# Opening of a conformer/attention block: x in eight wide transfers, true transposes, rstd at the read of the banks, shift and scale summed by one wide VectorE operation

## Chip, cores and metric

One core of one Trainium2 chip runs the kernel. The metric is the device time of one launch in microseconds (us), lower being better. The time given for the kernel before is the median of three runs; one more execution was taken with the hardware profiler.

## What is computed

The layer normalises x (512 tokens x 2048 features), modulates it by shift and scale that come from a conditioning vector c, multiplies it with one wide weight matrix, runs a convolution branch and an attention branch on the results, and merges them. The part that the change touches is the first five lines:

```python
c_act = jax.nn.silu(c)
mod = c_act @ w_ada[l] + b_ada[l]                 # 2048 -> 3 * 2048
shift, scale, gate = jnp.split(mod, 3, axis=-1)
h = rms_norm(x, g_pre[l]) * (1.0 + scale[:, None, :]) + shift[:, None, :]
p = h @ w_in[l]
cv, cg, cz, q, k, v, az, m_conv, m_attn = jnp.split(p, offsets, axis=-1)
y_conv = conv_branch(cv, cg, cz, conv_w[l], conv_b[l], cn_g[l], cn_b[l], w_conv_out[l])
y_attn = attn_branch(q, k, v, az, l, lam_q1[l], lam_k1[l], lam_q2[l], lam_k2[l], subln_g[l], w_attn_out[l])
merged = jax.nn.sigmoid(m_conv) * y_conv + jax.nn.sigmoid(m_attn) * y_attn
out = merged @ w_o[l]
x = x + gate[:, None, :] * rms_norm(out, g_post[l])
```

`rms_norm` divides each token by the root of its mean square (here rstd is one over that root) and multiplies by a vector over the features. Everything is float32.

## The kernel before

**Products.** A float32 operand is held as two parts of a shorter type, hi and lo, and a product is three matmuls (hi hi, hi lo, lo hi), issued by `mm3` (L161 to L167; the profile lists them under L163). `split` makes the parts: ScalarE rounds to hi (L141), VectorE takes the difference lo (L142). Features lie on the partitions, the 512 tokens in the free dimension; `h[k]` is the hi and lo tile of the 128 features of tile k, of 16.

**Opening, up to the first `pv` matmul.** x comes as tokens x features in 16 tiles of 128x512 (L93 to L95). `squares` (L211) sums the squares of the tiles, half on ScalarE and half on VectorE; `scales` (L221) makes rstd of two token tiles and a diagonal matrix with it. `norm_x` (L232) multiplies a piece of x with that diagonal on TensorE (L236), which transposes and scales it at once, and ScalarE copies the result from the PSUM bank to `xn` (L239): 64 products and 64 copies of 128x128.

Shift and scale of a few features at a time, a group, come from `ada` (L257). `GROUPS` (L47) gives seven of them: first column, width, and how many of the 16 parts of the sum over c TensorE takes; VectorE takes the rest. `ada_load` (L249) loads columns of `w_ada`, shift and scale apart, 512 KB each. On TensorE a part is a matmul with the vector c as the stationary operand, into `pa` (L273); on VectorE it is a scaled add into `acc` (L276, L278). Small matmuls turn the sums so that features lie on the partitions (`pm`, L288 to L294), and then ScalarE forms `hf` = xn * scale + shift (L305) and `split` makes `h[k]`.

`conv_gemm` (L318) multiplies the tiles `h[k]` of a group with the 2048 columns of the GLU part of `w_in`: one, one, two, two, two, four and four tiles k (kt0, kt1, kt2, kt4, kt6, kt8 and kt12 in what follows, by their first tile). The bank of each output tile (`pc`) goes to `part`: by a ScalarE copy for kt0 (L337), by a VectorE add for the others (L339), 16 per block. So a block needs its group's shift and scale, and while it runs, the next group's are worked out. `interleave` (L173) writes the two in alternating order, `ST` (L45) saying in how many steps, and the rest of `norm_x` is spread over kt0.

**Order.** All DMAs are issued by SyncE, in order. Inside the `manual_schedule` block (L349 to L364) instructions keep the order written; elsewhere a scheduler of the language orders each engine's program at build time. Each engine runs its program strictly in that order, so an instruction that waits holds everything behind it.

**Pools.** `page` (L69) hands out 59 tiles of 128x512; the loads of `ada` share seven tiles of 128x1024 (`AR`).

Behind the opening come the convolution taps on VectorE, attention, the gates and the two projections, whose TensorE program is the same before and after the change.

Of the kernel before, what the change touches and what calls it, by code (L numbers as in the profile page):

```python
# [977 lines left out]
```

## Time and profile before

| what | before |
|---|---|
| median of three runs | 1447.2 us (1445.42 to 1449.49) |
| profiled execution, its own time | span 1448.4 us |
| TensorE (PE) busy | 1413.6 us, 98% |
| VectorE (DVE) busy | 1053.0 us, 73% |
| ScalarE (ACT) busy | 534.2 us, 37% |
| bytes moved by DMA | 238.62 MB, 165 GB/s in the mean |
| first conv product / first `pv` product | 33.05 us / 258.29 us |

The profile gives busy time for each engine, and for TensorE the clock that it was granted as a share of full speed. A busy TensorE may be a slow one; matmuls overlap, so the distance from one start to the next is what one costs. Time lies on the path only where the engine that ends last waits for it.

### The profile page before, as it was taken

The numbers are of one execution on the slowest core, as the hardware profiler recorded it, in microseconds if no ns is written. First come the engines' busy times: TensorE is split into PE (matmuls) and PEld (weight loads), VectorE is DVE, ScalarE is ACT, GpSimd is POOL, SyncE is SP. The second block draws the span as 40 slices with busy tenths as digits, with TensorE's granted clock in tenths as the row PEclk, the third lists the DMA queues.
The fourth block names the chain that finished last, engine by engine and source line by source line (L and its number), as shares of the span: only waits on it lengthen the run. The fifth ranks groups of instructions, "written<-read, shape, count | busy, mean of one in ns | idle before, by whom it ended". The sixth has DMA issues, their size and how long they took to land.

```text
span 1448.4 us, 20732 instructions
## 1 busy us (share of the span) xinstructions
PE 1413.6 (98%) x8191; PEld 1200.4 (83%) x8191; DVE 1053.0 (73%) x1720; ACT 534.2 (37%) x901; POOL 1.8 (0%) x8
## 2 busy tenths in 40 slices
PE   4999999999999999999999999999999999999997
PEld 4776778787777877688999999999998888888885
DVE  4466785988888888588997888877767448656645
ACT  4622233223444244434544444444445323222230
POOL 0000000000000000000000000000000000000000
PEclk9999999999999999999999999999999999999999
DMA  9878653232223323124654555533369647267543
GB/s 285 264 255 291 215 167 130 88 131 87 66 81 102 102 67 109 66 95 135 209 165 160 187 178 191 188 121 132 126 226 349 224 137 233 95 207 243 189 145 145
DMA packets 178466, 238.62 MB, mean 165 GB/s; under 512 B 7793, under 2 KB 118722, under 8 KB 177474
## 3 DMA queue, kind: packets, MB, share of 16 engines
q1 hardware_dynamic: 178370, 237.31, 49.5%
q8 instruction: 64, 1.05, 0.3%
q14 instruction: 32, 0.26, 0.1%
HBM read 210.02 MB, written 27.26 MB: 164 GB/s over the span
## 4 chain that ended last, share of the span: by engine, by line
PE 93%; DVE 3%; DMA 1%; ACT 1%; issue 1%; SPq 0%; DVEq 0%; ACTq 0%
PE pc L163 12%; PE pw L163 12%; PE py_ya L163 6%; PE py_yc L163 6%; PE pv L163 6%; PE pg_k L163 6%; PE pg_q L163 5%; PE pg_az L163 5%; PE x_ma L163 5%; PE x_mc L163 5%; PE y_mc L163 3%; PE z_mc L163 3%; PE z_ma L163 3%; PE y_ma L163 3%; PE x_cz L163 2%; PE y_cz L163 2%
## 5 line engine op out<-in xcount | busy, mean ns | idle before, releaser
L468 DVE SCALAR_TENSOR_TENSOR cacc<-u,cw,cacc 128x511 f32<-128x511 f32 (+14 forms) x240 | 164.4, 729 | 0.0
L163 PE MATMUL pc<-hh,wh_c 128*128 128x512 f32 x256 | 102.9, 408 | 1.1 <-ACT hh L141 1.1
L163 PE MATMUL pc<-hh,wl_c 128*128 128x512 f32 x256 | 101.0, 398 | 1.5 <-DVE wl_c L142 1.4
L163 PE MATMUL pc<-hl,wh_c 128*128 128x512 f32 x256 | 101.7, 397 | 0.0
L339 DVE TENSOR_TENSOR part<-pc,part 128x512 f32<-128x512 f32 x96 | 66.0, 691 | 46.9 <-PE pc L163 45.8
L163 PE MATMUL pw<-wh_o,mh 128*128 128x512 f32 x224 | 89.0, 397 | 0.0
L163 PE MATMUL pw<-wh_o,ml 128*128 128x512 f32 x224 | 87.3, 390 | 0.0
L163 PE MATMUL pw<-wl_o,mh 128*128 128x512 f32 x224 | 87.2, 389 | 0.0
L141 ACT CAST wh_c<-wr_c 128x1024 fp32r<-128x1024 f32 (+1 forms) x36 | 34.6, 960 | 112.5 <-PE pc L163 85.6
L141 ACT CAST wh_o<-wr_o 128x1024 fp32r<-128x1024 f32 x28 | 29.5, 1053 | 104.5 <-PE pw L163 93.0
L163 PEld LDWEIGHTS pc<-hh,wh_c 128*128 128x128 f32 x256 | 49.0, 192 | 17.9 <-issue 3.3
L856 DVE SCALAR_TENSOR_TENSOR accg<-adag,cact,accg 128x512 f32<-128x512 f32 x60 | 45.0, 750 | 24.0 <-DMA adag<-in_w_ada_dram 22.8
L163 PEld LDWEIGHTS pc<-hh,wl_c 128*128 128x128 f32 x256 | 49.1, 192 | 15.7 <-issue 2.5
L142 DVE TENSOR_TENSOR wl_o<-wr_o,wh_o 128x1024 fp32r<-128x1024 f32 x28 | 34.2, 1221 | 34.0 <-ACT wh_o L141 34.0
L163 PEld LDWEIGHTS pc<-hl,wh_c 128*128 128x128 f32 x256 | 49.3, 192 | 10.2 <-issue 0.4
L163 PE MATMUL pv<-wh_v,hh 128*128 128x512 f32 x128 | 51.2, 400 | 0.9 <-DVE part L339 0.9
L142 DVE TENSOR_TENSOR wl_c<-wr_c,wh_c 128x1024 fp32r<-128x1024 f32 (+1 forms) x36 | 39.7, 1104 | 16.5 <-ACT wh_c L141 16.4
L163 PE MATMUL pg_q<-hh,wh_q 128*128 128x512 f32 x128 | 51.1, 399 | 0.0
L163 PE MATMUL pg_k<-hh,wl_k 128*128 128x512 f32 x128 | 51.1, 399 | 0.0
L163 PE MATMUL pg_q<-hl,wh_q 128*128 128x512 f32 x128 | 50.9, 397 | 0.0
L163 PE MATMUL pg_az<-hl,wh_az 128*128 128x512 f32 x128 | 50.7, 396 | 0.0
L163 PE MATMUL pv<-wl_v,hh 128*128 128x512 f32 x128 | 50.6, 395 | 0.0
(358 smaller groups left out, 4312.7 us busy)
## 6 DMA issues: line engine op xcount, KB each, us to landing
ada<-in_w_ada_dram SPq DMA_DIRECT2D x64, 512.0 KB, 6.1
wr_ma<-in_w_in_dram SPq DMA_DIRECT2D x16, 1024.0 KB, 5.5
wr_mc<-in_w_in_dram SPq DMA_DIRECT2D x16, 1024.0 KB, 5.0
adag<-in_w_ada_dram SPq DMA_DIRECT2D x32, 512.0 KB, 4.2
wr_o<-in_w_o_dram SPq DMA_DIRECT2D x16, 1024.0 KB, 5.1
wr_c<-in_w_in_dram SPq DMA_DIRECT2D x28, 512.0 KB, 5.0
wr_v<-in_w_in_dram SPq DMA_DIRECT2D x8, 1024.0 KB, 5.2
wr_q<-in_w_in_dram SPq DMA_DIRECT2D x8, 1024.0 KB, 5.3
```

Of the source, the lines that this page charges most:

```text
L141: nc.scalar.copy(hi, src)
L142: i = nc.vector.tensor_tensor(lo, src, hi.bitcast(F32), op=ALU.subtract)
L163: mm = nc.tensor.matmul(ps, a[p], b[q], start=start and i == 0, stop=stop and i == 2, skip_group_check=more)
L339: nc.vector.tensor_tensor(part[i], ps[f], part[i], op=ALU.add)
L468: paced(nc.vector.scalar_tensor_tensor(cvo[t][:, s:], u[t][:, :S - s], wj, cvo[t][:, s:], op0=ALU.mult, op1=ALU.add))
L856: nc.vector.scalar_tensor_tensor(acc, raw[:, k, :], s1, acc, op0=ALU.mult, op1=ALU.add)
```

## The change

- x comes in eight transfers of 128x1024 (512 KB), and the two row loads (`b_ada`, `g_pre`) behind them.
- `turn` transposes a piece of x with the identity; a broadcast of rstd over the partitions, made once by four small matmuls with a matrix of ones (`rsb`), is multiplied in by VectorE when it reads the bank: 64 transposes, four to a bank, and 16 VectorE operations of 128x512.
- A load of `ada` is one tile with shift and scale side by side, filled by two transfers of 256 KB. VectorE's part of a sum is one operation over both, twice as wide.
- `GROUPS`: the groups at columns 256 and 768 go from 16 parts on TensorE to none, that at 1024 from 12 to 8.
- Tiles that belong together (x, most of `xn`, hi and lo of `h`, `ya`, `mg`, `mgs`) are pairs of a pool of their own. The pages go from 59 to 27, the load tiles from 7 to 6.
- The small loads for the convolution and for lambda go behind the last load of `ada`.

```diff
-NPAGE = 59
+NPAGE = 27
-AR = 7
-ST = (3, 6, 6, 6, 13, 10)
-GROUPS = ((0, 128, 16), (128, 128, 16), (256, 256, 16), (512, 256, 16), (768, 256, 16),
-          (1024, 512, 12), (1536, 512, 0))
+AR = 6
+ST = (3, 10, 10, 10, 13, 10)
+GROUPS = ((0, 128, 16), (128, 128, 16), (256, 256, 0), (512, 256, 16), (768, 256, 0),
+          (1024, 512, 8), (1536, 512, 0))
...
     for t in range(NT):
-        for j in range(4):
-            nc.sync.dma_start(out=xs[t][j], in_=x2[t * P:(t + 1) * P, j * 512:(j + 1) * 512])
-        if t == 0:
-            row_load(b_ada2[:2 * D], V_BADA, 32)
-            row_load(g_pre[0], V_GPRE, 16)
+        for j in range(2):
+            nc.sync.dma_start(out=xs[t][j], in_=x2[t * P:(t + 1) * P, j * 1024:(j + 1) * 1024])
+    row_load(b_ada2[:2 * D], V_BADA, 32)
+    row_load(g_pre[0], V_GPRE, 16)
...
+        rsb = ap.tile([P, S], F32, name="rsb")
+        prs = mbank("prs0")
         def scales(t0):
...
             for t in (t0, t0 + 1):
-                diag[t] = ap.tile([P, P], F32, name=f"diag_{t}")
-                nc.vector.tensor_scalar_mul(diag[t], ident, r[:, t - t0:t - t0 + 1])
-
-        def norm_x(j, ts):
-            for t in ts:
-                pt = gbank(f"pxt_{t}_{j}")
-                for i in range(4):
-                    nc.tensor.matmul(pt[:, i * P:(i + 1) * P], xs[t][j][:, i * P:(i + 1) * P], diag[t],
-                                     start=True, stop=True)
-                for i in range(4):
-                    nc.scalar.copy(xn[4 * j + i][:, t * P:(t + 1) * P], pt[:, i * P:(i + 1) * P])
+                diag = ap.tile([P, P], F32, tag="diag", bufs=2, name=f"diag_{t}")
+                nc.vector.tensor_scalar_mul(diag, ident, r[:, t - t0:t - t0 + 1])
+                nc.tensor.matmul(prs[:, t * P:(t + 1) * P], ones, diag, start=True, stop=True)
+            ts = slice(t0 * P, (t0 + 2) * P)
+            nc.scalar.copy(rsb[:, ts], prs[:, ts])
+
+        def turn(ks, ts):
+            for k in ks:
+                if pxt[k] is None:
+                    pxt[k] = gbank(f"pxt_{k}")
+                for t in ts:
+                    nc.tensor.transpose(pxt[k][:, t * P:(t + 1) * P], xs[t][k // 8][:, k % 8 * P:(k % 8 + 1) * P],
+                                        ident)
+
+        def norm_x(ks):
+            for k in ks:
+                nc.vector.tensor_tensor(xn[k], pxt[k], rsb, op=ALU.mult)
...
         def ada_load(k0, nk, c0, width):
-            raws = []
+            raw = ap.tile([P, nk, 2, width], F32, tag="ar", bufs=AR, name=f"ada_{c0}_{k0}")
             for a in range(2):
-                raw = ap.tile([P, nk, width], F32, tag="ar", bufs=AR, name=f"ada_{a}_{c0}_{k0}")
-                nc.sync.dma_start(out=raw, in_=ada_v[:, k0:k0 + nk, a * D + c0:a * D + c0 + width])
-                raws.append(raw)
-            return raws
+                last_load[0] = nc.sync.dma_start(out=raw[:, :, a, :],
+                                                 in_=ada_v[:, k0:k0 + nk, a * D + c0:a * D + c0 + width])
+            return raw
...
-            nk, nb, kb = 1024 // width, width // P, c0 // P
+            nk, nb, kb = 512 // width, width // P, c0 // P
-            acc = [page(f"acc{a}_{c0}") for a in range(2)] if npe < KT else None
+            acc = ap.tile([P, 2, width], F32, tag="acc", bufs=1, name=f"acc_{c0}") if npe < KT else None
...
-                            nc.vector.scalar_tensor_tensor(acc[a][:, :width], raw, cact[:, kk:kk + 1],
-                                                           acc[a][:, :width], op0=ALU.mult, op1=ALU.add)
+                        nc.vector.scalar_tensor_tensor(acc, raw[:, kk - k0, :, :], cact[:, kk:kk + 1], acc,
+                                                       op0=ALU.mult, op1=ALU.add)
...
         with tc.manual_schedule(engines={mybir.EngineType.PE, mybir.EngineType.Activation, mybir.EngineType.DVE}):
...
+            for t in range(NT):
+                squares(t)
+                turn(range(4), (t,))
+                if t % 2:
+                    scales(t - 1)
+            rows()
+            norm_x(range(4))
             group = ada(*GROUPS[0])
+            next(group)
+            turn(range(4, 8), range(NT))
+            norm_x(range(4, 8))
...
+        with tc.issue_after(last_load[0].ins):
+            for src, r0, n in ((conv_b[0], V_CB, 8), (cn_g[0], V_CNG, 8), (cn_b[0], V_CNB, 8), (subln_g[0], V_SUB, 1)):
```

The change also moves instructions that its lines don't name. VectorE around kt1, before: the part sums of kt1 (`part`, each out of a bank `pc`), the differences of the weights (`wl_c`), and no sum over c.

```order
L339 TENSOR_TENSOR part_415<-pc_0_0_3_636,part_415 128x512
L142 TENSOR_TENSOR wl_c_1_1_763<-wr_c_1_1_760,wh_c_1_1_762 128x512
L339 TENSOR_TENSOR part_462<-pc_0_1_0_671,part_462 128x512
L339 TENSOR_TENSOR part_464<-pc_0_1_1_672,part_464 128x512
L339 TENSOR_TENSOR part_466<-pc_0_1_2_673,part_466 128x512
L339 TENSOR_TENSOR part_468<-pc_0_1_3_674,part_468 128x512
L142 TENSOR_TENSOR wl_c_0_0_815<-wr_c_0_0_812,wh_c_0_0_814 128x1024
L284 COPY accp_747<-pa_620 128x256
```

For shift and scale VectorE only copies TensorE's sum here (`accp`). VectorE between the first products of kt0 and kt1 after the change: `acc_567` is the sum of group 2 (columns 256), `ada_2`, `ada_4` ... are its loads, `xn<-pxt` the new multiplies.

```order
L146 TENSOR_TENSOR wl_c_1_0_353<-wr_c_1_0_350,wh_c_1_0_352 128x512
L305 TENSOR_SCALAR acc_567<-ada_0_568,cact 128x512
L307 SCALAR_TENSOR_TENSOR acc_567<-ada_0_568,cact,acc_567 128x512
L307 SCALAR_TENSOR_TENSOR acc_567<-ada_2_573,cact,acc_567 128x512
L146 TENSOR_TENSOR wl_c_1_1_525<-wr_c_1_1_522,wh_c_1_1_524 128x512
L260 TENSOR_TENSOR xn_137<-pxt_427,rsb 128x512
L307 SCALAR_TENSOR_TENSOR acc_567<-ada_2_573,cact,acc_567 128x512
L307 SCALAR_TENSOR_TENSOR acc_567<-ada_4_604,cact,acc_567 128x512 x2
L260 TENSOR_TENSOR xn_138<-pxt_457,rsb 128x512
```

The sums over c of group 2 now stand among the splits and multiplies that kt0 and kt1 need. In kt1 they stand among its part sums too:

```order
L369 TENSOR_TENSOR part_493<-pc_1_0_0_655,part_493 128x512
L307 SCALAR_TENSOR_TENSOR acc_567<-ada_12_650,cact,acc_567 128x512
L369 TENSOR_TENSOR part_495<-pc_1_0_1_656,part_495 128x512
L307 SCALAR_TENSOR_TENSOR acc_567<-ada_12_650,cact,acc_567 128x512
L369 TENSOR_TENSOR part_497<-pc_1_0_2_657,part_497 128x512
L369 TENSOR_TENSOR part_499<-pc_1_0_3_658,part_499 128x512
L307 SCALAR_TENSOR_TENSOR acc_567<-ada_14_681,cact,acc_567 128x512
L146 TENSOR_TENSOR wl_c_1_1_702<-wr_c_1_1_699,wh_c_1_1_701 128x512
L307 SCALAR_TENSOR_TENSOR acc_567<-ada_14_681,cact,acc_567 128x512
```

So a bank of kt1 is read only when the sum ahead of it has its load. TensorE ahead of kt2 after the change, where `pa_732` is group 3's sum (columns 512) and `pm_566` turns group 2's:

```order
L324 MATMUL pm_566<-ones,acc_567 128x1 x4
...
L302 MATMUL pa_732<-ada_0_733,c_126 32x256 x4
L302 MATMUL pa_732<-ada_2_740,c_126 32x256 x4
L302 MATMUL pa_732<-ada_4_785,c_126 32x256 x4
L302 MATMUL pa_732<-ada_6_792,c_126 32x256 x4
L302 MATMUL pa_732<-ada_8_837,c_126 32x256 x4
L302 MATMUL pa_732<-ada_10_844,c_126 32x256
```

These are 21 of group 3's 32 matmuls; before, ten of the 32 stood ahead of kt2. A matmul of float32 operands is two rows in the trace.

## Rows read from the trace of the kernel before

**Rows 1.** Head of the page, busy time (section 1) and the last chain by engine (section 4).

```profile
span 1448.4 us, 20732 instructions
...
PE 1413.6 (98%) x8191; PEld 1200.4 (83%) x8191; DVE 1053.0 (73%) x1720; ACT 534.2 (37%) x901; POOL 1.8 (0%) x8
...
PE 93%; DVE 3%; DMA 1%; ACT 1%; issue 1%; SPq 0%; DVEq 0%; ACTq 0%
```

**Rows 2.** Waits of PE from 258 us on: engine, line, releaser: total us, times, longest.

```profile
PE pot L553 <- DVE on L549: 1.4, 5, 0.3
PE pv L163 <- DVE part L339: 0.9, 1, 0.9
```

**Rows 3.** PE timeline: start, us, engine, line, operation, count, idle time before and its releaser.

```profile
30.91 1.07 PE L273 MATMUL pa<-ada,c 128*32 128x128 f32 x30 [0.50 <-DMA ada<-in_w_ada_dram]
33.05 1.92 PE L163 MATMUL pc<-hh,wh_c 128*128 128x512 f32 x4 [1.07 <-ACT hh L141]
34.77 0.63 PE L163 MATMUL pc<-hl,wh_c 128*128 128x512 f32 x1
...
40.30 0.40 PE L163 MATMUL pc<-hh,wh_c 128*128 128x512 f32 x1
...
73.74 1.20 PE L163 MATMUL pc<-hh,wh_c 128*128 128x512 f32 x4
...
126.78 1.92 PE L273 MATMUL pa<-ada,c 128*32 128x512 f32 x16
...
149.91 0.36 PE L294 MATMUL pm<-ones,acc 128*128 128x1 f32 x2
...
191.05 0.50 PE L163 MATMUL pc<-hh,wl_c 128*128 128x512 f32 x1 [1.43 <-DVE wl_c L142]
...
258.29 0.47 PE L163 MATMUL pv<-wh_v,hh 128*128 128x512 f32 x1 [0.88 <-DVE part L339]
```

**Rows 4.** Windows of 20 us: busy us (instructions) of each engine, PEclk, DMA share, GB/s.

```profile
20.00:40.00 20.00, 15.95 (x181) 13.10 (x180) 6.76 (x25) 10.03 (x34) 0.00 (x0) 0.83 1.11 314
...
140.00:160.00 20.00, 20.00 (x90) 13.62 (x85) 8.02 (x14) 6.52 (x10) 0.00 (x0) 0.83 0.81 274
...
180.00:200.00 20.00, 18.57 (x82) 14.99 (x81) 19.64 (x28) 4.21 (x4) 0.00 (x0) 1.00 0.66 206
```

**Rows 5.** Groups by line and form, 0 to 260 us; the last one 33 to 75 us, PE.

```profile
L339 DVE TENSOR_TENSOR part<-pc,part 128x512 f32<-128x512 f32 x96 | 66.0, 691 | 46.9 <-PE pc L163 45.8
...
L142 DVE TENSOR_TENSOR wl_c<-wr_c,wh_c 128x1024 fp32r<-128x1024 f32 x28 | 34.1, 1222 | 2.0 <-ACT wh_c L141 1.9
...
L278 DVE SCALAR_TENSOR_TENSOR acc<-ada,cact,acc 128x512 f32<-128x512 f32 x36 | 25.3, 747 | 0.0
...
L273 PE MATMUL pa<-ada,c 128*32 128x256 f32 x192 | 12.8, 384 | 0.0
...
L118 DVE SCALAR_TENSOR_TENSOR xr_y<-xr_t,xr_y 128x2 f32<-128x2 f32 x6 | 1.0, 161 | 0.2
...
L236 PE MATMUL pxt<-diag,x 128*128 128x128 f32 x80 | 9.9, 277 | 0.0
```

**Rows 6.** Tile pt, transposes of attention: durations min/median/max in ns.

```profile
L533 PE MATMUL pt<-ident,t x80: 270/273/332, 351.7 to 612.2; 128*128 128x128 f32 x80
```

**Rows 7.** ACT timeline, the squares of x.

```profile
11.21 0.63 ACT L219 ACTIVATE xsq<-x 128x512 f32<-128x512 f32 x1 [0.63 <-DMA x<-in_x_dram]
...
12.55 0.63 ACT L219 ACTIVATE xsq<-x 128x512 f32<-128x512 f32 x1 [0.62 <-DMA x<-in_x_dram]
```

**Rows 8.** DVE timeline in kt8, where VectorE is full.

```profile
175.54 0.69 DVE L339 TENSOR_TENSOR part<-pc,part 128x512 f32<-128x512 f32 x1
176.15 1.22 DVE L142 TENSOR_TENSOR wl_c<-wr_c,wh_c 128x1024 fp32r<-128x1024 f32 x1
177.28 0.75 DVE L278 SCALAR_TENSOR_TENSOR acc<-ada,cact,acc 128x512 f32<-128x512 f32 x1
177.94 0.69 DVE L339 TENSOR_TENSOR part<-pc,part 128x512 f32<-128x512 f32 x1
```

More of the change, by code (lines that the diff above doesn't have):

```diff
@@ L70, in page, with pair_of @@
         return pp.tile([P, S], dt, tag="pg", name=name)
+    def pair_of(name, dt=F32R):
+        return pr.tile([P, 2, S], dt, tag="pr", name=name)
     ident = cpool.tile([P, P], F32, name="ident")
@@ L85, in hybrid_trunk @@
     nc.sync.dma_start(out=crow, in_=c[0].rearrange("(r q) -> r q", q=P))
-    xs = [[page(f"x_{t}_{j}") for j in range(4)] for t in range(NT)]
+    xs = [[pair_of(f"x_{t}_{j}", F32).rearrange("p a n -> p (a n)") for j in range(2)] for t in range(NT)]
     vrow = page("vrow")
@@ L204, in hybrid_trunk, with xpart @@
         nc.vector.memset(halves[64:, 1:2], 1.0)
-        xn = [page(f"xn_{kt}") for kt in range(KT)]
+        xn = []
+        for kt in range(0, KT - 4, 2):
+            g = pair_of(f"xn_{kt}", F32)
+            xn += [g[:, 0, :], g[:, 1, :]]
+        xn += [page(f"xn_{kt}") for kt in range(KT - 4, KT)]
         ss = small(KT, "xss")
-        diag = [None] * NT
+        def xpart(t, j):
+            return xs[t][j // 2][:, j % 2 * S:(j % 2 + 1) * S]
         def squares(t):
@@ L240, in norm_x, with turn_norm, rows @@
+        def norm_x(ks):
+            for k in ks:
+                nc.vector.tensor_tensor(xn[k], pxt[k], rsb, op=ALU.mult)
+        def turn_norm(ks):
+            for k in ks:
+                turn((k,), range(NT))
+                norm_x((k,))
                 yield
-        pv = mbank("pv")
-        nc.tensor.transpose(pv[:, :V_N0], vrow[:V_N0, :P], ident[:V_N0, :V_N0])
-        nc.vector.tensor_copy(vec[:, :V_N0], pv[:, :V_N0])
         bsc1 = cpool.tile([P, KT], F32, name="bsc1")
-        nc.vector.tensor_scalar_add(bsc1, vec[:, V_BADA + KT:V_BADA + 2 * KT], 1.0)
+        def rows():
+            pv = mbank("pv")
+            nc.tensor.transpose(pv[:, :V_N0], vrow[:V_N0, :P], ident[:V_N0, :V_N0])
+            nc.vector.tensor_copy(vec[:, :V_N0], pv[:, :V_N0])
+            nc.vector.tensor_scalar_add(bsc1, vec[:, V_BADA + KT:V_BADA + 2 * KT], 1.0)
@@ L265, in ada @@
             for k0 in range(0, KT, nk):
-                raws = ada_load(k0, nk, c0, width)
+                raw = ada_load(k0, nk, c0, width)
                 for kk in range(k0, k0 + nk):
                     on_pe = (kk + 1) * npe // KT > kk * npe // KT
-                    for a in range(2):
-                        raw = raws[a][:, kk - k0, :]
-                        if on_pe:
+                    if on_pe:
+                        for a in range(2):
                             m = 2 * a + n % 2
-                            nc.tensor.matmul(pa[32 * m:32 * m + 32, :width], c32[:, kk, :], raw,
+                            nc.tensor.matmul(pa[32 * m:32 * m + 32, :width], c32[:, kk, :], raw[:, kk - k0, a, :],
@@ L293, in ada @@
                         nc.tensor.matmul(col, accp[:, bs], halves[:, a:a + 1], start=True, stop=False)
-                    nc.tensor.matmul(col, acc[a][:, bs], ones[:, :1], start=not npe, stop=True)
+                    nc.tensor.matmul(col, acc[:, a, bs], ones[:, :1], start=not npe, stop=True)
             sh = small(4, f"sh_{c0}")
@@ L833, in hybrid_trunk @@
     for k in range(8):
-        hi, lo = page(f"yah_{k}", F32R), page(f"yal_{k}", F32R)
+        g = pair_of(f"ya_{k}")
+        hi, lo = g[:, 0, :], g[:, 1, :]
         fetch(f"yah{k}", hi.bitcast(F32))
@@ L867, in hybrid_trunk @@
             k = 2 * j + f
-            g = page(f"mg_{k}")
+            if k % 2 == 0:
+                mgp = pair_of(f"mg_{k}", F32)
+            g = mgp[:, k % 2, :]
             fetch(f"ma{k}", g)
```

59 lines of the change are left out of this document (27 added, 32 removed).

## Prediction

> **What bounds the kernel now.** I read the head of the page first: TensorE is busy for 1413.6 of the span's 1448.4 us, and the chain that ended last is 93% TensorE [rows 1]. So time is won where TensorE's program gets shorter or loses a wait. Its waits come next: from 258 us to the end the two largest groups, both on VectorE, are 1.4 and 0.9 us [rows 2]. Behind 258 us TensorE goes from one instruction to the next, and their order from there on is the same in both kernels. So the change acts by the moment at which the first `pv` product starts, 258.29 us before [rows 3]; the rest follows at the same distance. In the main part VectorE's sums of the gate move a little earlier; I cost that at nothing, for the 2.3 us of waits there are all that it could touch.
>
> The opening decides, and there the table of windows says more than the averages [rows 4]. From 20 to 40 us TensorE is busy 15.95 of 20 us, at a clock of 0.83. From 140 to 160 it is never idle, but the clock is 0.83 again: a conv matmul takes 0.23 us from start to start at 40.30 and 0.43 at 34.77 [rows 3], at the levels of 2.4 and 1.2 GHz. From 180 to 200 VectorE is full (19.64 of 20) and TensorE loses 1.43 us to a `wl_c` [rows 3, 4]. The change takes work from TensorE and gives VectorE more, so the question is whether VectorE has room at the place where it gets it.
>
> **Transposes.** Before, 64 products with a diagonal. 40 of them lie behind 33 us, where TensorE is the chain, as 80 rows of 128 columns [rows 5], so each makes two. After, there are 64 true transposes, 32 of them behind the first conv product. The trace has 80 such transposes elsewhere, for 80 instructions, one row each, 273 ns for one by itself [rows 6]. Packed, the diagonal rows start 0.112 us apart and I take 0.11 for the others, an estimate by the equal width. That is 80 x 0.112 - 32 x 0.11 = 5.4 us off TensorE; if a transpose took two passes it would be 1.8. I take 5.4, since [rows 6] is the same operation. The 64 ScalarE copies to `xn` go, and ScalarE is not the bound. In their place VectorE gets 16 multiplies of 128x512 out of a bank, at the price of the part sum, which reads a bank too: 691 ns [rows 5].
>
> **Shift and scale on TensorE.** The two groups of 256 columns that leave TensorE had 64 rows each at 12.8 us / 192 = 0.067 us [rows 5]: 4.3 us a group. The 512 group gives up 16 rows, 1.9 us by the batch at 126.78 [rows 3]. The VectorE sums need short rows instead, about eight a group at the 0.11 us of 149.91 [rows 3]: 0.9.
>
> **Shift and scale on VectorE.** Groups 2 and 4 (columns 256 and 768) need 16 operations of 128x512 each, shift and scale in one, at 747 ns [rows 5]. In the 512 groups a wide operation covers 128x1024. The trace has none: from below 1222 ns (a difference of that width, [rows 5]), from above two of the old, 1494. I take 1.25, near the row of the same width. Group 6 falls from 32 x 0.747 = 23.9 to 16 x 1.25 = 20.0 us.
>
> **x and the loads.** Eight transfers of 512 KB carry the bytes of sixteen of 256. ScalarE's squares, one for every second tile, waited for x at 11.21 and 12.55 us [rows 7]: 512 KB in 1.34 us, 391 GB/s. Wider can gain little there, and the last scale is ready some 2 us sooner because the row loads go behind x. The first conv product can start at about 31 instead of 33.05, as half of the second group's columns arrive at 30.91 [rows 3], with the same bytes ahead. The loads of shift and scale go from 64 of 512 KB to 128 of 256 KB; by the x tiles that costs nothing, and the other end is rival D. The Trainium skill ("DMA: Bandwidth & Descriptors", section Bandwidth) has the rule to batch transfers to at least 1 MiB for 75% of peak; 391 GB/s at 256 KB doesn't agree with a loss of that size. The small loads that move behind the last column load feed nothing that TensorE needs before 213 us: nothing.
>
> **The new wait.** Up to the second block of two (kt2, 73.74 us before [rows 3]) TensorE by its own sum would be early: 73.74 - 33.05 = 40.7 us, minus 5.4 (transposes), minus 4.3 (group 2), plus 22 rows of group 3 that now come before kt2 (1.5) and short ones (0.4) is 32.9; from 31 that ends at 64. But group 2's sums now stand in VectorE's program between the splits of `w`, the `xn` multiplies and the part sums, and each waits in order for its transfer. The second of these loads has landed when the queue has moved what lies behind 30.91 us: 1.05 MB of group 1, 0.52 and 0.52 of group 2, 0.26 of weights, in all 2.35 MB, at the window's 314 GB/s [rows 4] 7.5 us: 38.4. From there to the last split that kt2 needs first, VectorE's order has 54 instructions: 14 sums x 0.747, 5 splits, 8 `xn`, 3 differences and 16 part sums of one width, 32 x 0.691, a split of 1024 at 1.22, one copy and six short ones, 7 x some 0.2 (161 ns in [rows 5]): 10.5 + 22.1 + 1.2 + 1.4 = 35.2. Back to back they overlap, and by the distance of starts (0.61 for a part sum, 1.13 for the split, 0.66 for a sum [rows 8]) it is 9.2 + 19.5 + 1.1 + 1.4 = 31.2. The part sums come spaced by TensorE's products, so I take a value near the upper, 34.3: kt2 starts at **72.7**, 1.0 earlier than before instead of 10. From below it is 69; if VectorE waits in turn for the products, 78.
>
> **Behind kt2,** each stage by its own edits: kt2 loses the 22 group-3 rows, 1.6 us. kt4 loses group 4's 64 rows (4.3) and pays 0.9 and some 1.0 of waiting behind VectorE's new sums: 2.4. kt6 loses the 16 rows, 2.0. kt8 loses the wait of 1.43 at 191.05 [rows 3], group 6 being lighter: 1.5. Sum 7.5. Against it: if TensorE waits for VectorE ahead of kt2, its clock may fall once more. A window with a fall has 0.83 [rows 4], 0.17 x 20 = 3.4 us; I take half, 1.7. The Trainium skill ("TensorE: Matmul & The Clock Gate", Part 1) says that an idle array goes to 1.2 GHz; the row at 34.77 behind a wait of 1.07 agrees, the one at 191.05 behind 1.43 doesn't.
>
> Sum: 1.0 + 7.5 - 1.7 = 6.8 us less. The profiled span of 1448.4 would become 1441.6; it lies 1.2 above the median of the runs, so the median becomes **1440.4 us**. About 0.3% (4.3 us) is what a measurement of this kernel tells from no change: faster is below 1442.9, slower above 1451.5.
>
> **Rivals.** (A) VectorE keeps up: its loads come earlier and it overlaps with itself fully. Then kt2 starts at 64 and no clock falls: 9.7 + 7.5 = 17.2 less, 1430. For it: VectorE is busy only 6.76 of 20 us from 20 to 40 [rows 4]. Against it: 54 instructions in order fill 31 us at least, 69.
>
> (B) Slower. VectorE waits in order for each of group 2's eight loads, 1.5 us each, with `xn` multiplies and part sums held behind them, and TensorE runs out of banks: kt2 at 72.7 + 12 = 84.7, 11 later; the clock falls over a whole window (3.4): 11 + 3.4 - 7.5 = 6.9 more, 1454. It decides from kt2's start on: above 83 the sum is slower by 0.3%. For it: the queue is near full (314 GB/s [rows 4]), and one tile fewer holds these loads (6 for 7), so that a late reader delays a later load. Against it: eight loads of 0.52 MB are 13 us of transfer, in 34.
>
> (C) No net change: kt2 at 78, 4.3 later, so 7.5 - 4.3 - 1.7 = 1.5 less, 1445.7.
>
> (D) Halved transfers cost more. [...] By rows, at most the 0.67 us of an x tile for each of 64 added transfers, in a queue that is near full for a third of them: 14 us, 7 of it eaten by the gain, 1454. The 391 GB/s speak against it.
>
> **How the numbers follow.** The forecast has 0.46, of which 0.43 is faster (its own range is 1436 to 1444, kt2 from 69 to 76); A 0.15, C 0.24, B 0.11, D 0.04. Faster 0.58, same 0.27, slower 0.15. The range goes from A, 1430, to C's upper end, 1449 (kt2 at 81); B, D and the tail of A are left out.
>
> **What would show it.** In the profile after: 64 transposes of one row each; 64 rows of 256 columns instead of 192; the wide sum at 1.2 to 1.3 us; kt2's first product at 69 to 76 us, VectorE busy over 17 of 20 us from 40 to 60 with TensorE waiting there for `xn`, `wl_c` or a bank; the first `pv` near 251.5. It is wrong if TensorE doesn't wait between 40 and 73 (A), if VectorE waits for loads there (B), if x lands later than before (D), or if the time behind the first `pv` changes by more than 1 us.

## The result, and the profile after

The changed kernel takes 1434.0 us (median of four runs, 1433.55 to 1436.9), the kernel before, run beside it, 1446.8: a ratio of 0.9916 with a 95% interval of 0.9902 to 0.9930, so 12.8 us less where 6.8 were forecast. The sign and the range held, and the size fell between the forecast and rival A. The profiled execution has a span of 1435.1 us against 1448.4 [rows 1], 13.3 less. Its head, with the chain that ended last:

```profile
span 1435.1 us, 20362 instructions
...
PE 1397.3 (97%) x7999; PEld 1189.5 (83%) x7999; DVE 1080.9 (75%) x1750; ACT 522.1 (36%) x839; POOL 1.8 (0%) x8
...
PE 90%; DVE 5%; DMA 2%; ACT 1%; issue 1%; SPq 0%; DVEq 0%; ACTq 0%
```

TensorE is the chain as before; it is busy for 16 us less, VectorE for 28 more. The timeline of TensorE in the changed kernel, at the places that answer to [rows 3] (start, length, engine, line, operation, count, wait before it):

```profile
30.91 1.43 PE L167 MATMUL pc<-hp,wh_c 128*128 128x512 f32 x5 [1.00 <-ACT hp L145]
...
38.43 0.72 PE L167 MATMUL pc<-hp,wh_c 128*128 128x512 f32 x2 [0.84 <-DVE xn L260]
...
47.25 1.47 PE L255 MATMUL pxt<-ident,x 128*128 128x128 f32 x12
...
60.04 1.33 PE L167 MATMUL pc<-hp,wh_c 128*128 128x512 f32 x4 [0.53 <-DVE part L369]
...
63.92 2.37 PE L302 MATMUL pa<-ada,c 128*32 128x256 f32 x40
...
67.46 1.42 PE L167 MATMUL pc<-hp,wh_c 128*128 128x512 f32 x5
...
136.29 0.28 PE L323 MATMUL pm<-halves,accp 128*128 128x1 f32 x2
...
136.65 0.36 PE L323 MATMUL pm<-halves,accp 128*128 128x1 f32 x2
136.88 0.36 PE L324 MATMUL pm<-ones,acc 128*128 128x1 f32 x2
...
140.17 0.57 PE L323 MATMUL pm<-halves,accp 128*128 128x1 f32 x2
140.59 0.56 PE L324 MATMUL pm<-ones,acc 128*128 128x1 f32 x2
...
154.79 0.50 PE L167 MATMUL pc<-hp,wl_c 128*128 128x512 f32 x1 [1.30 <-DVE wl_c L146]
...
243.67 0.47 PE L167 MATMUL pv<-wh_v,hp 128*128 128x512 f32 x1 [0.87 <-DVE part L369]
...
925.51 0.36 PE L167 MATMUL x_mc<-t4h,wh_mc_a 128*128 128x256 f32 x1 [1.13 <-DVE tb_mc L718]
```

The first conv product starts at 30.91 (33.05 before), the block kt2 at 67.46 (73.74), the first `pv` product at 243.67 (258.29): the opening gives 14.6 us. From there to the end the kernel takes 1191.4 us, before 1190.1. Of the 1.3 given back, 1.13 is one wait at 925.51, whose releaser on VectorE itself waited for a load of weights:

```profile
923.81 1.23 DVE L705 TENSOR_TENSOR ws_mc<-wr_mc,wr_mc 128x1024 f32<-128x1024 f32 x1 [2.91 <-DMA wr_mc<-in_w_in_dram]
```

Its load was issued at 915.17 and had not landed before 923.8. The same wait appears in the profiles of two of the kernels below (e3, e5) and in none of the others, while all have this part of the TensorE program in common: a late transfer of single executions, and this one took 1436.9 us, the longest of the four. In nine of the twelve profiles of the experiments the end lies 1190.1 to 1190.4 us behind the first `pv` product, as before; in e3, e5 and e7, each with a late wait, it is 1191.8 to 1192.5. So my sentence that the main part costs nothing holds for the kernel, not for this profile. By the letter of my own sign of being wrong (a change of more than 1 us behind the first `pv`) this profile meets it, with 1.3.

By stages, from the start of each block's first product in the two TensorE timelines:

| stage | before | after | change | forecast |
|---|---|---|---|---|
| start to kt0 | 33.05 | 30.91 | -2.1 | -2 |
| kt0 and kt1 | 40.69 | 36.55 | -4.1 | +1 |
| kt2 | 27.15 | 24.42 | -2.7 | -1.6 |
| kt4 | 27.74 | 24.67 | -3.1 | -2.4 |
| kt6 | 36.79 | 34.97 | -1.8 | -2.0 |
| kt8 | 47.90 | 47.18 | -0.7 | -1.5 |
| kt12 to the first `pv` | 44.97 | 44.97 | 0.0 | 0 |

The windows of 20 us (columns as in [rows 4]):

```profile
20.00:40.00 20.00, 16.51 (x187) 13.17 (x188) 14.03 (x31) 8.71 (x16) 0.00 (x0) 1.00 1.08 317
40.00:60.00 20.00, 18.36 (x89) 13.94 (x87) 19.95 (x36) 8.56 (x15) 0.00 (x0) 1.00 0.82 266
...
140.00:160.00 20.00, 18.70 (x74) 15.16 (x75) 16.66 (x24) 7.96 (x11) 0.00 (x0) 0.87 0.55 176
160.00:180.00 20.00, 20.00 (x90) 16.57 (x89) 19.41 (x22) 4.21 (x4) 0.00 (x0) 1.00 0.89 292
```

From 40 to 60 us VectorE is full (19.95) and TensorE is busy 18.36 of 20: the new wait is there, as forecast, for `part` and `wl_c`, as at 60.04. From 20 to 40 the clock is 1.00, which was 0.83 in [rows 4]. From 140 to 160 it is 0.87 and the fall is still in kt6. VectorE's timeline shows the length of that wait:

```profile
34.15 0.49 DVE L305 TENSOR_SCALAR acc<-ada,cact 128x512 f32<-128x512 f32 x1 [1.37 <-DMA ada<-in_w_ada_dram]
...
36.42 0.75 DVE L307 SCALAR_TENSOR_TENSOR acc<-ada,cact,acc 128x512 f32<-128x512 f32 x1 [0.99 <-DMA ada<-in_w_ada_dram]
...
49.80 5.12 DVE L369 TENSOR_TENSOR part<-pc,part 128x512 f32<-128x512 f32 x8
...
65.69 1.22 DVE L146 TENSOR_TENSOR wl_c<-wr_c,wh_c 128x1024 fp32r<-128x1024 f32 x1
```

Its sums wait for loads at 34.15 and 36.42 us. From 36.42 on VectorE runs without a break of over 0.6 us to the split of 128x1024 at 65.69 that kt2 needs. That the chain passes through VectorE here is also seen in the one stretch that holds both blocks, kt0's first product to kt2's:

```profile
30.91:67.46 36.55, 32.88 (x212) 23.85 (x213) 33.47 (x59) 18.69 (x32) 0.00 (x0) 1.00 0.89 288
```

TensorE is busy for 32.88 of 36.55 us. The costs of the new operations, by line and form up to 250 us:

```profile
L307 DVE SCALAR_TENSOR_TENSOR acc<-ada,cact,acc 128x1024 f32<-128x1024 f32 x22 | 28.1, 1277 | 0.1
L307 DVE SCALAR_TENSOR_TENSOR acc<-ada,cact,acc 128x512 f32<-128x512 f32 x30 | 22.3, 744 | 1.1 <-DMA ada<-in_w_ada_dram 1.0
...
L260 DVE TENSOR_TENSOR xn<-pxt,rsb 128x512 f32<-128x512 f32 x16 | 10.1, 680 | 0.0
```

The wide sum takes 1277 ns (1250 taken), the sum of 128x512 takes 744, and `xn` 680. On TensorE:

```profile
L255 PE MATMUL pxt<-ident,x 128*128 128x128 f32 x64 | 11.3, 334 | 5.2 <-DMA x<-in_x_dram 5.1 <-DVE xn L260 0.2
...
L302 PE MATMUL pa<-ada,c 128*32 128x256 f32 x64 | 4.7, 384 | 0.6 <-DVE wl_c L146 0.6
```

64 transposes make 64 rows, and the 256-column rows are 64 instead of the 192 of [rows 5].

### The profile page after: what moved, and what is told of

Same layout as the page of the kernel before. It is cut to its first block, busy times and chain, and to the rows that moved or that the text cites. A ratio compares the mean times of both kernels' runs of the same rounds, so it can differ in the third digit from the quotient of the medians.

```text
span 1435.1 us, 20362 instructions
## 1 busy us (share of the span) xinstructions
PE 1397.3 (97%) x7999; PEld 1189.5 (83%) x7999; DVE 1080.9 (75%) x1750; ACT 522.1 (36%) x839; POOL 1.8 (0%) x8
## 4 chain that ended last, share of the span: by engine, by line
PE 90%; DVE 5%; DMA 2%; ACT 1%; issue 1%; SPq 0%; DVEq 0%; ACTq 0%
PE pw L167 12%; PE pc L167 11%; PE py_ya L167 6%; PE py_yc L167 6%; PE pv L167 6%; PE pg_az L167 5%; PE pg_q L167 5%; PE pg_k L167 5%; PE x_ma L167 5%; PE x_mc L167 4%; PE z_ma L167 3%; PE y_ma L167 3%; PE y_mc L167 3%; PE z_mc L167 3%; PE x_cz L167 2%; PE y_cz L167 2%
## 5 line engine op out<-in xcount | busy, mean ns | idle before, releaser
L167 PE MATMUL pc<-hp,wh_c 128*128 128x512 f32 x512 | 159.9, 397 | 3.0 <-DVE part L369 1.2
L167 PE MATMUL pw<-wh_o,mgs 128*128 128x512 f32 x448 | 140.6, 393 | 0.0
L167 PEld LDWEIGHTS pc<-hp,wh_c 128*128 128x128 f32 x512 | 95.6, 190 | 29.0 <-issue 2.7
L167 PE MATMUL pc<-hp,wl_c 128*128 128x512 f32 x256 | 99.0, 396 | 2.1 <-DVE wl_c L146 2.1
L167 PEld LDWEIGHTS pw<-wh_o,mgs 128*128 128x128 f32 x448 | 84.1, 188 | 18.9 <-ACT fsq L932 0.7
L167 PE MATMUL pw<-wl_o,mgs 128*128 128x512 f32 x224 | 87.2, 389 | 0.0
L167 PE MATMUL pv<-wh_v,hp 128*128 128x512 f32 x256 | 82.8, 397 | 0.9 <-DVE part L369 0.9
L167 PE MATMUL pg_q<-hp,wh_q 128*128 128x512 f32 x256 | 82.7, 398 | 0.0
L167 PE MATMUL pg_az<-hp,wh_az 128*128 128x512 f32 x256 | 81.5, 395 | 0.0
L167 PE MATMUL pg_k<-hp,wh_k 128*128 128x512 f32 x256 | 80.1, 392 | 0.0
```

Of the source, the lines that this page charges most:

```text
L167: mm = nc.tensor.matmul(ps, a[p], b[q], start=start and i == 0, stop=stop and i == 2, skip_group_check=more)
```

## Experiments

Two theories stood after this. V: up to kt2 VectorE's program sets the time, and behind it TensorE's rows do. T: TensorE's rows count everywhere and VectorE hides. All kernels are edits of the changed kernel unless it says otherwise, and each ratio is to the kernel before, run beside it (the changed kernel's is 0.9916, 0.9902 to 0.9930).

**e1: TensorE's shares as before.**

```diff
-(256, 256, 0), (512, 256, 16), (768, 256, 0), (1024, 512, 8)
+(256, 256, 16), (512, 256, 16), (768, 256, 16), (1024, 512, 12)
```

> The changed kernel, but with TensorE's share of the sums as before (columns 256 and 768: all 16 parts, 1024: 12). Theory V (VectorE's program in order sets the time up to kt2, TensorE's rows set it behind): up to kt2 TensorE takes back 64 rows (4.3 us) but no longer waits (3.7 us of waits between 31 and 67 us in the changed kernel), so kt2 starts at 65 to 68 instead of 67.46; kt4 takes back 64 rows less the short ones, +3; kt6 16 rows, +1.9. First pv at 246 to 249 instead of 243.67, time 1436 to 1440. Theory T (TensorE's rows count everywhere, VectorE hides): +4.3 + 4.3 + 1.9 - 0.9 = 9.6, first pv at 253, time about 1443.6. If the change of shares were worth nothing: 1434.

Measured: 1437.4 us, 0.9929 (0.9914 to 0.9944); kt2 at 65.94, first `pv` at 247.91. From kt0's first product to kt2's:

```profile
31.29:65.94 34.65, 34.65 (x265) 25.24 (x265) 25.75 (x45) 18.28 (x31) 0.00 (x0) 1.00 0.89 292
```

TensorE is busy throughout, and the stretch is 1.9 us shorter than in the changed kernel, though 64 rows of group 2 are back in it. So V, which expected kt2 at 65 to 68, the first `pv` at 246 to 249 and 1436 to 1440 us. Eight rows of group 3 (0.5 us) moved behind kt2's start here; the rest, some 1.4 us, is what group 2's shift to VectorE loses where it stands. The shares pay in kt4 (24.67 against e1's 31.87, part of which is a fall of the clock at 116 to 120 us). The whole opening is 4.2 us longer in this profile; the intervals of the timed runs overlap.

**e2: transposes as two-pass products.**

```diff
-nc.tensor.transpose(pxt[k][...], xs[t][k // 8][...], ident)
+nc.tensor.matmul(pxt[k][...], xs[t][k // 8][...], ident, start=True, stop=True)
```

> The changed kernel, but each of the 64 transposes a plain fp32 product with the identity: two rows each instead of one, same numbers. Theory V: of 64 x 0.11 = 7 us the 32 behind the first conv product (3.5 us) are hidden up to kt2, because VectorE is busy without a break from 36.4 to 63 us; the 16 just ahead of the first sums delay the first conv product by up to 1.8. kt2 at 67.5 to 69, time 1434 to 1435.5. Theory T: 48 rows more on the path, 5.3 us, kt2 at 72.8, time 1439.

Measured: 1439.4 us, 0.9938 (0.9921 to 0.9955). kt0 at 33.48, kt2 at 70.84, first `pv` at 248.29. The rows double:

```profile
L255 PE MATMUL pxt<-ident,x 128*128 128x128 f32 x128 | 21.3, 333 | 3.9 <-DMA x<-in_x_dram 3.7 <-DVE xn L260 0.2
```

T's time came out (1439), but not its place: it had kt2 at 72.8. V missed both, kt2 by 1.8 us and the time by 3.9. The interval overlaps the changed kernel's. Of the 3.4 us at kt2, 2.6 are there at the first conv product, where V gave up to 1.8. Only 0.8 come in kt0 and kt1, so there the 32 rows (3.5 us) are hidden for the most part, as V has it. Another 1.2 us come behind kt2, where the edit changes nothing; they weren't followed up. In this profile the clock also falls from 20 to 28 us, where the transposes ahead of the first sums run. Such a fall stands in e1 and e11 too, where it goes with a first conv product only 0.4 and 0.5 us later than in the kernels that they are edits of (31.29 against 30.91, 31.55 against 31.05); so some 2 of the 2.6 us are likely the rows', by an estimate from these.

**e3: shift and scale summed apart.**

```diff
-nc.vector.scalar_tensor_tensor(acc, raw[:, kk - k0, :, :], cact[:, kk:kk + 1], acc, ...)
+for a in range(2):
+    nc.vector.scalar_tensor_tensor(acc[:, a, :], raw[:, kk - k0, a, :], cact[:, kk:kk + 1], acc[:, a, :], ...)
```

> The changed kernel, but VectorE sums shift and scale in two operations of half the width instead of one. By the rows: 128x512 at 0.744 becomes two of 128x256 at about 0.48 (an estimate from half the width and the fixed part that 744 and 1277 ns show, 0.21), +0.22 each; 128x1024 at 1.277 becomes two of 0.747, +0.22. Theory V: 14 sums stand ahead of kt2, so kt2 at 67.5 + 3.1 = 70.5; in kt4 and kt6 VectorE is 18.2 to 18.7 of 20 us busy, and 16 and 24 more of 0.22 us do not fit wholly: 1 to 3 more. First pv at 247 to 250, time 1437 to 1440. Theory T: VectorE has room, nothing changes, 1434.

Measured: 1443.5 us, 0.9969 (0.9954 to 0.9984), clear of the changed kernel; kt2 at 72.83, first `pv` at 249.97. The prices were right, the distance was not: kt2 comes 2.3 us behind V's 70.5.

```profile
L309 DVE SCALAR_TENSOR_TENSOR acc<-ada,cact,acc 128x512 f32<-128x512 f32 x44 | 30.8, 743 | 0.0
L309 DVE SCALAR_TENSOR_TENSOR acc<-ada,cact,acc 128x256 f32<-128x256 f32 x60 | 25.9, 477 | 1.2 <-DMA ada<-in_w_ada_dram 1.2
```

In the changed kernel one operation does what two do here: two of 477 ns for one of 744, two of 743 for one of 1277. V has the sign and the place of the first `pv`, but the time is 3 us above its range, of which this profile's waits behind the opening (1.2 and 0.8 us in `x_mc` and `x_cz`) show a part. Two windows show the fall of the clock that the forecast had as 1.7 us:

```profile
40.00:60.00 20.00, 15.85 (x79) 13.05 (x80) 19.77 (x43) 8.27 (x14) 0.00 (x0) 1.00 0.74 241
60.00:80.00 20.00, 19.90 (x100) 13.24 (x99) 14.10 (x26) 5.41 (x7) 0.00 (x0) 0.74 0.74 240
```

VectorE is full, TensorE sits idle for 4 of 20 us (its longest wait, for a `wl_c`, is 3.1), and its clock is 0.74 in the next 20. The fall that I expected ahead of kt2 comes here, with longer waits than the changed kernel has. By the medians the wide operation is worth more than any other part that was undone; its interval touches e2's, which ends at 0.9955.

**e4, e5, e9: the transfers of x.** e4 has sixteen tiles of 256 KB with the row loads behind the first four, e5 the same with the row loads behind x, e9 the wide tiles as two transfers of 64 partitions each.

```diff
-for j in range(2):
-    nc.sync.dma_start(out=xs[t][j], in_=x2[t * P:(t + 1) * P, j * 1024:(j + 1) * 1024])
+for j in range(4):
+    nc.sync.dma_start(out=xs[t][j // 2][:, j % 2 * 512:(j % 2 + 1) * 512], in_=x2[t * P:(t + 1) * P, j * 512:(j + 1) * 512])
```

> The changed kernel, but x in sixteen transfers of 256 KB and the row loads behind the first four, as before. If VectorE's sums, which wait for their loads at 34 and 36 us, set kt2: the first conv product comes up to 2 us later (33), but the bytes ahead of the sums are the same, so kt2 stays at 67.5 to 68 and the time at 1434 to 1434.5. If the start of the first product counts: all later by 2, 1436. If the width of a transfer matters by itself, x lands later still, over 2.

> The changed kernel, but x in sixteen transfers of 256 KB; the two row loads stay behind x. With the row loads in the middle as well, group 2's first load was ready for VectorE at 36.65 us instead of 34.15, and kt2 started at 70.2 instead of 67.5. Theory W (width of x): the same here, 36 to 37 and kt2 at 69.5 to 70.5, time 1436 to 1437. Theory R (the row loads among x hold the queue): as in the changed kernel, 34 to 34.5, kt2 at 67.5, time 1434.

> The changed kernel, but x in sixteen transfers of 256 KB that keep rows of 4 KB: each wide transfer as two, of 64 partitions each. Narrow tiles (256 KB, rows of 2 KB) moved 3.42 MB in the first 14 us where the wide ones moved 4.22, and kt2 came 2.2 us later. Theory S (what counts is how much a transfer carries, with some eight under way at a time): like the narrow ones, 3.4 to 3.6 MB in 14 us, kt2 at 69.5 to 70.5, time 1437. Theory L (what counts is the length of the rows): like the wide ones, 4.1 to 4.3 MB, kt2 at 67 to 68, time 1434.

Measured: e4 1437.4 us, 0.9934 (0.9915 to 0.9953), kt2 at 70.21; e5 1437.9, 0.9935 (0.9914 to 0.9956), kt2 at 69.68; e9 1442.2, 0.9962 (0.9952 to 0.9973), kt2 at 75.17. VectorE's first sum of group 2 in e5:

```profile
36.32 0.49 DVE L306 TENSOR_SCALAR acc<-ada,cact 128x512 f32<-128x512 f32 x1 [1.40 <-DMA ada<-in_w_ada_dram]
```

36.32 us, 2.2 later than in the changed kernel, with the row loads where the change puts them, and kt2 follows by as much: Theory W, and the last branch of e4's, so it is the transfers of x. The ratios of e4 and e5 don't show it by themselves, since their intervals overlap the changed kernel's; the places in the profiles do, and both kernels agree. e9 came out later than both of its theories had it. The windows from 2 to 8 and 8 to 14 us, the last two columns the DMA share and GB/s; first the changed kernel:

```profile
2.00:8.00 6.00, 1.37 (x5) 0.90 (x5) 2.33 (x9) 1.68 (x6) 0.61 (x1) 1.00 0.90 286
8.00:14.00 6.00, 1.24 (x5) 0.84 (x5) 3.99 (x20) 1.45 (x4) 0.00 (x0) 1.00 1.02 415
```

e5:

```profile
2.00:8.00 6.00, 1.37 (x5) 0.89 (x5) 1.63 (x7) 1.67 (x6) 0.61 (x1) 1.00 0.74 214
8.00:14.00 6.00, 1.12 (x4) 0.72 (x4) 2.58 (x9) 1.45 (x4) 0.00 (x0) 1.00 1.01 355
```

e9:

```profile
2.00:8.00 6.00, 1.34 (x5) 0.89 (x5) 1.63 (x7) 0.96 (x4) 0.61 (x1) 1.00 0.92 220
8.00:14.00 6.00, 1.08 (x4) 0.71 (x4) 2.31 (x8) 2.17 (x6) 0.00 (x0) 1.00 1.04 234
```

The wide form moves (286 - 214) x 6 + (415 - 355) x 6 = 0.8 MB more than e5 by 14 us, which is some 2 us at these rates; all that stands behind x in the queue comes later by as much. SyncE's timeline shows it too, by the first loads of columns, in the changed kernel and in e5:

```profile
8.84 9.05 SPq L281 DMA_DIRECT2D ada<-in_w_ada_dram  x8
```

```profile
14.59 5.99 SPq L282 DMA_DIRECT2D ada<-in_w_ada_dram  x8
```

The eight wide transfers are all issued by 5.4 us, while in e5 SyncE waits for transfers of x to land before it has issued the last of the sixteen. e9 shows that rows of 4 KB alone don't bring it: 234 GB/s. But its transfers also take 64 partitions instead of 128, and it differs from e5 in kind: in the first window the DMA engines are busy 0.92 at 220 GB/s, in e5 0.74 at 214. So whether a transfer's size, the number under way or its partitions decide is open.

**e8, e11: the loads of 512 columns in one transfer.** The 32 loads of the two last groups are 512 KB each, in e11 on top of e6 (below).

```diff
+if nk == 1:
+    if a == 0:
+        last_load[0] = nc.sync.dma_start(out=raw[:, 0, :, :], in_=ada_w[:, k0, :2, c0:c0 + width])
+    continue
```

> The changed kernel, but the 32 loads of the two 512-column groups are one transfer of 512 KB each instead of two of 256 KB. If a transfer's size costs nothing at 256 KB: same stages within 0.3 us, time 1434. If each transfer has a cost of its own (the rival on halved transfers: up to 0.67 us for each of 32, a third of them on the path): kt6's wait for its loads (0.4 us) goes and the loads of kt6 land earlier, 2 to 7 less, 1427 to 1432.

> The kernel with the merged sums (e6), and the loads of the two 512-column groups as one transfer of 512 KB each. With the merged sums no clock falls in kt6, so that what the size of a transfer does there can be seen alone: kt6's stage was 29.86 us with one wait of 0.8 for a load. If the size costs nothing: 29.5 to 30, time 1430 to 1431. If the loads are what kt6 waits for and 512 KB come sooner: the wait of 0.8 goes, 29.1, time 1429.5.

Measured: e8 1434.5 us, 0.9913 (0.9891 to 0.9935); e11 1430.8, 0.9882 (0.9867 to 0.9896), against e6's 1430.55. No difference in time. Rival D falls for these loads: halving them costs nothing that the timed runs show, unlike x. The stage kt6 by itself is 1.1 us shorter in e11's profile than in e6's (28.8 and 29.9), but e10 and e12, with halved loads, have 30.5 and 29.2, so one profile of each doesn't settle that. The wait of 0.8 us for a load that e11's expectation puts into kt6 stands at 66.95 us, ahead of kt2; in kt6 e6 has none.

**e6: fewer one-column products in kt6,** where both engines sum (columns 1024).

```diff
-accp = page(f"accp_{c0}")
-nc.vector.tensor_copy(accp[:, :width], pa[:, :width])
+if npe == KT:
+    accp = page(f"accp_{c0}")
+    nc.vector.tensor_copy(accp[:, :width], pa[:, :width])
+else:
+    for a in range(2):
+        hs = slice(64 * a, 64 * a + 64)
+        nc.vector.tensor_tensor(acc[hs, a, :], pa[hs, :width], acc[hs, a, :], op=ALU.add)
...
-if npe:
-    nc.tensor.matmul(col, accp[:, bs], halves[:, a:a + 1], start=True, stop=False)
```

> The changed kernel, but where a group is summed on both engines (columns 1024) VectorE adds TensorE's bank to its own sum, so that 8 one-column products do where 16 did: 16 rows less in the series ahead of the clock's fall in kt6, two VectorE operations of 64x512 (at 0.69) for one copy. Theory V: TensorE is the chain in kt6, 16 rows at 0.11 to 0.21 us, 1.8 to 3.4 less; if the shorter series also keeps the clock at 1.00, 3.4 more. kt6's stage 30 to 33.5 instead of 34.97 us, time 1428 to 1432. Rival: VectorE's adds are late by more than the rows save, or the clock falls elsewhere: 1434.

Measured: 1430.55 us (1430.26 to 1431.59), 0.9888 (0.9871 to 0.9906), 3.4 us less than the changed kernel, as V expected (1428 to 1432). All four runs lie below all four of the changed kernel, while the intervals of the two ratios just touch (0.9906 and 0.9902). TensorE's timeline, the short products (two more stand just ahead of them) and the first of kt8:

```profile
137.35 1.62 PE L327 MATMUL pm<-ones,acc 128*128 128x1 f32 x14
...
146.39 2.13 PE L167 MATMUL pc<-hp,wh_c 128*128 128x512 f32 x8
```

The stage from 116.53 to 146.39 is 29.9 us, 34.97 in the changed kernel. There 32 short rows run from 136.29 to 140.59, and in the middle of them, with TensorE never idle, two such rows go from 0.23 us (136.65 to 136.88) to 0.42 (140.17 to 140.59). Here 16 rows are over before that, and the clock stays:

```profile
120.00:140.00 20.00, 19.96 (x93) 13.29 (x92) 15.43 (x21) 1.04 (x1) 0.00 (x0) 1.00 1.03 362
140.00:160.00 20.00, 18.58 (x80) 14.56 (x80) 19.92 (x26) 8.91 (x12) 0.00 (x0) 1.00 0.76 245
```

The stage gains 5.1 us and the median 3.4. In the changed kernel's profile, its slowest execution, the clock is at half for 6.8 us in kt6 (from 138.4 on), which costs 3.4; in e1, e4, e5, e8 and e9 for 3.4 us only, which costs 1.7. With that shorter fall the gain would be 3.4, an estimate from these profiles.

That the short rows bring the fall is likely, not shown. Of ten profiles with 32 such rows in kt6 nine have a fall in them or within 1 us behind them, and the four with 16 (e6, e10, e11, e12) have none. The exception is e3, which has all 32:

```profile
140.00:160.00 20.00, 18.18 (x100) 14.36 (x99) 15.60 (x28) 9.02 (x12) 0.00 (x0) 1.00 0.72 250
```

**e7, e10, e12: how much of group 2 TensorE takes.** Of its 16 parts 8 in e7, 4 in e10 and all 16 in e12, the last two on top of e6.

```diff
-(256, 256, 0)
+(256, 256, 8)
```

> The changed kernel, but TensorE takes 8 of the 16 parts of the sum for columns 256. VectorE has 8 sums of 0.66 us less and one copy more ahead of kt2, TensorE 32 rows of 0.067 and 8 short rows of 0.11 more (3.0 us). Theory V: VectorE's 31 us fall to 26, then TensorE's own program of 32.9 + 3.0 us from 31 decides: kt2 at 66 to 67, 0.5 to 1.5 earlier, time 1432.5 to 1433.5. Theory T: TensorE's rows come on top, kt2 at 70.5, 1437. If the loads decide (VectorE waits for them whatever it does): kt2 at 67.5, 1434.

> The kernel with the merged sums (e6), and TensorE takes 4 of the 16 parts of the sum for columns 256. VectorE saves 4 sums of 0.66 us for two adds of 64x256 at some 0.4; TensorE gets 16 rows of 0.067. Theory V: VectorE's path to kt2 is 1.8 us shorter, TensorE's own is 1.1 longer at 63.8 + 1.1: kt2 at 65 to 66.5 instead of 67.5, time 1428.5 to 1430. If the balance is already reached, as with half the parts on TensorE, where kt2 stayed at 67.65: 67 to 68 and 1430.5 to 1431.

> The kernel with the merged sums (e6), and group 2 (columns 256) whole on TensorE again, as in e1, while columns 768 stay on VectorE. In e1 TensorE was busy for all of the 34.65 us from its first conv product to kt2, in the changed kernel for 32.88 of 36.55. Theory V: kt2 comes 1 to 1.9 us earlier (65.5 to 66.5), kt2's own stage pays up to 0.5 for eight rows more of group 3, the rest is as in e6: 0.5 to 1.5 less, 1429 to 1430. Theory T (the shift of group 2 to VectorE is a gain in its full 4.3 us): 4.3 more, 1435.

Measured: e7 1439.3 us, 0.9944 (0.9924 to 0.9964), kt2 at 67.65; e10 1434.6, 0.9909 (0.9894 to 0.9924), kt2 at 69.54; e12 1430.0 (1429.11 to 1430.31), 0.9876 (0.9858 to 0.9894), kt2 at 66.35. kt0 to kt2 in e7, and its short products there:

```profile
30.52:67.65 37.13, 36.12 (x252) 25.98 (x252) 29.40 (x51) 18.18 (x31) 0.00 (x0) 1.00 0.83 269
```

```profile
L324 PE MATMUL pm<-ones,acc 128*128 128x1 f32 x8 | 1.4, 250 | 0.0
L323 PE MATMUL pm<-halves,accp 128*128 128x1 f32 x8 | 1.4, 239 | 0.0
```

The same stretch in e12:

```profile
31.71:66.35 34.64, 34.64 (x265) 25.25 (x265) 25.76 (x45) 18.17 (x31) 0.00 (x0) 1.00 0.90 295
```

A share between the engines brought nothing. e10 has both ends beside it: its kt2 comes 2.0 us later than e6's (67.50, nothing of group 2 on TensorE) and 3.2 later than e12's (all of it), and its ratio is the highest of the three, though the intervals still touch. e7's kt2 comes where the changed kernel's does, in the place that its expectation gave to the loads (67.5), while V had 66 to 67; the 5 us that its median is longer lie mostly behind kt2 in the profile, among them a wait of 1.0 us for a load in kt6 and one of 1.2 for ScalarE in the main part, and the intervals overlap.

A share costs TensorE the rows and two sets of short products (2.8 us busy in e7), and it takes VectorE's work away only in part: TensorE is busy for 36.12 us in e7, for 34.64 without a gap in e12. e10 missed its forecast by 3 us in kt2's start. Its TensorE is busy 36.85 us in that stretch, 4 more than in the changed kernel. That is in the rows of 256 columns: 68 stand ahead of kt2 instead of 42, sixteen of group 2 and ten more of group 3, and they are busy for 7.2 us instead of 3.0. The sixteen come in runs of four, busy for 0.63 us each; e12's 98 come in runs of 8 to 34 and are busy for 6.6. e12 came out as V had it, 0.6 us below e6, which the intervals don't tell apart. It is the fastest kernel of this study by its median, 18.6 us below the kernel before, which ran beside it at 1448.6.

Not undone by any run: the multiply by rstd at the read of the banks, with the 64 copies that it takes off ScalarE, the pools, `ST`, and the place of the small loads. What each of these is worth is open.

## Why the prediction was right or wrong

- **What bounds the kernel**: right. The opening decides, the rest follows at its distance but for one late transfer. But the opening gave twice what was forecast: kt2 at 67.46 lies outside the 69 to 76 that I named as a sign, and the first `pv` at 243.67 is 7.8 us ahead of the 251.5.
- **Transposes**: the rows are one each and follow at (1.47 - 0.27) / 11 = 0.11 us (the twelve at 47.25). The place was wrong. I put their worth into kt0 and kt1; in e2, 2.6 of the 3.4 us at kt2 arise ahead of the first conv product, some of it by the clock, and VectorE hides most of the rest. (With two passes the sum is 1.9, not 1.8.)
- **TensorE's own program** up to kt2: 32.9 forecast, 32.88 busy, in part by luck. The 40.7 us that the sum starts from hold the fall of the clock that the kernel before has at the start of kt0, some 1.7 us that the changed kernel doesn't pay. And busy time among waits is longer than the program's own: e12's 34.64 us without a gap, less its 56 more rows of 256 columns at 0.067, leave some 31 (an estimate). As VectorE came last, neither mattered to kt2. One microsecond of that fall, in the kernel before:

```profile
34.00:35.00 1.00, 1.00 (x4) 0.81 (x3) 0.41 (x1) 0.00 (x0) 0.00 (x0) 0.50 0.93 313
```

- **x and the loads**: the step "wider can gain little there" failed. I read 391 GB/s off two rows in the middle of x [rows 7]; more than half of the difference lies ahead of 8 us, where the sixteen transfers move 214 GB/s and the eight 286. I had put the 2 us on the row loads, and e5 shows that they matter little: its first sum of group 2 comes 0.3 us ahead of e4's (36.32 and 36.65). The rule of the Trainium skill on batching ("DMA: Bandwidth & Descriptors", section Bandwidth), which I set aside by that row, points the right way for x; for the column loads e8 and e11 show nothing of it. Group 2's second load was ready at 36.42 instead of 38.4.
- **VectorE's 54 instructions**: the mechanism was right, the term was mis-sized. 36.42 to 67.46 is 31.0 us; the sum by the distance of starts was 31.2, by mean durations 35.2, and I took 34.3 because I thought that the products would space the part sums. But VectorE was behind, TensorE waited for it to empty the banks (0.53 us at 60.04), and it ran back to back (eight part sums in 5.12 us at 49.80), so that the distance of starts was the price. This (3.3 us) and the 2.0 of the loads are the 5.2 between 72.7 and 67.46.
- **The clock**: the term of 1.7 us failed. In the changed kernel no fall comes between the first conv product and kt2, the waits there being 0.84 us at most; one comes in e3, whose waits are longer, up to 3.1. The window from 20 to 40 us even lost the falls that it has in the kernel before (0.83).
- **Behind kt2**: 8.3 us for 7.5. kt2 and kt4 gave 1.8 more than forecast, and kt8 0.8 less, since the wait of 1.43 at 191.05 came back as 1.30 at 154.79, for a `wl_c` again, although group 6 is lighter.
- **Rivals**: A gave the time to within 4 us, nearer than the forecast, but not by its mechanism: VectorE didn't keep up (19.95 of 20 us), and kt2 came 3.5 us behind A's 64. B's waits for loads are 1.4 and 1.0 us, twice, not eight times. D is refuted for the column loads, as far as time shows, by e8 and e11, while its kind of cost exists for x.

So the span is 1435.1 where 1441.6 was forecast: 5.2 us at kt2, 0.8 behind it and 1.7 of a fall that didn't come, less 1.3 in the main part, are 6.4 of these 6.5.

## What to carry to other kernels

Price an engine that becomes the bound by the distance between its starts when it runs back to back: VectorE's 54 instructions took 31.0 us here, 31.2 by starts and 35.2 by durations. Where a sum is shared between two engines, count what joins the shares and how the rows then lie: neither share that was tried here beat giving all to one engine. And look at a stage's clock together with what the engine issued before it: 16 short rows less went with 5.1 us in their stage, where their own time is some 1.8.

## What was not expected

- The clock fell while TensorE was never idle, in the middle of 32 one-column rows, in kernels before and after; with 16 it did not (e6: 1.00 from 120 to 160 us). One kernel with 32, e3, kept its clock as well. In the changed kernel's timeline two of these rows take 0.23 us from start to start at 136.65 and 0.42 at 140.17.
- The opening up to 28 us is one program on TensorE in the changed kernel and in e1, yet e1's clock from 20 to 40 us is 0.83 and the changed kernel's is 1.00; e11 and e6 differ in the same way (0.83 and 1.00). So the program alone doesn't decide on a fall there. e1's first conv product comes 0.4 us later (31.29).
- Sixteen transfers of 256 KB were slower at the program's start than eight of 512, e9's with half the partitions slower yet, and the same halving made no difference in time for the column loads in kt6 and kt8.
